# One encoder layer with a Fourier mixer and a gated convolutional FFN on one core: first weight sums by accumulating DMA, subtractions moved from GpSimd to VectorE, earlier weight folds, fewer transfers in the down projection, and another split of the last norm

## The chip, the cores and the metric

The kernel runs on one core of one Trainium2 chip. The metric is the device time of one execution in microseconds, the median of several runs.

The engines go by the names of the profile: PE is TensorE (matmuls), DVE is VectorE, ACT is ScalarE, POOL is GpSimd, SP is the engine that only issues transfers. Each runs its own list of instructions in order and waits on semaphores where it needs another's result. A transfer is issued from SP's, ACT's or POOL's list and then runs by itself; only those issued from POOL can add to what stands in the destination ("accumulating").

## What is computed

The input x is 1024 positions by 1024 channels, float32, batch 1, one layer:

```python
def reference(x, ...):
    h = layer_norm(x, emb_ln_g, emb_ln_b)
    mix = fourier_mixer(h, fn_w_in, fn_b_in, fn_w_out, fn_b_out)
    h = layer_norm(DEEPNORM_ALPHA * h + mix, ln_tok_g, ln_tok_b)
    ffn = conv_ffn(h, ff_w_up, ff_conv_w, ff_conv_b, ff_w_down)
    return layer_norm(DEEPNORM_ALPHA * h + ffn, ln_ffn_g, ln_ffn_b)

def fourier_mixer(x, w_in, b_in, w_out, b_out):
    h = (x @ w_in + b_in).reshape(bsz, s, FN_GROUPS, FN_GROUP_DIM)
    f = jnp.fft.fft2(h, axes=(1, 3), norm="ortho").real
    return f.reshape(bsz, s, FN_WIDTH) @ w_out + b_out

def conv_ffn(x, w_up, conv_w, conv_b, w_down):
    h = depthwise_conv(x @ w_up, conv_w, conv_b)      # 3 taps over positions
    g, v = jnp.split(h, 2, axis=-1)                   # 2816 columns each
    return (jax.nn.silu(g) * v) @ w_down
```

## The kernel before

**Numbers in two pieces.** Each float32 operand of a matmul is split into a high part and a low part, both in the type float32r. `split` is a cast on ACT (high) and a subtraction `lows` on DVE or POOL (source minus high), and `mm3` multiplies in three passes: low × high, high × low, high × high (lines 190, 192, 194). So every product needs two operands, each with a high and a low part, and a low part is a tensor_tensor over the whole operand.

**Stages.** (1) Norm of x, transposes, the input weights with the transform over channels folded in, and the first products. (2) The transform over positions: `dft_cos` and `dft_sin` multiply with tables `ct` and `sn`. Their results come as banks `bp` and `bq` of PSUM and are split into `pte`, `pt` and `qt`. The output weights are used as sums and differences of mirrored columns ("folds"): `fold_load` fetches two pieces `w1` and `wd`, `fold_sums` negates `wd` on ACT and lets two accumulating transfers from POOL add the other piece to each, and `fold_split` splits the result into `wf`. A last piece, the weights' end rows with the biases, is `wee_f`, cast to `wee`. (3) For four row blocks t of positions, `out_sin` and `out_cos` multiply with the folded weights, `out_ln` adds the residual and takes the norm of row blocks t and t + 4 (statistics on DVE, a power on POOL, called `z10rs` and so on, and the centring), and `out_turn` transposes into `v` (PE), with gain and bias applied by ACT, or half by DVE where `both` is set. (4) The up projection: 22 column tiles j, each as seven products in the manner of Strassen, `prod(j, i)` with operands `a{i}_{j}` (weights: the columns `wr` and their sums `s`) and `b{i}` (activations: `v` and their differences `s1v`, `s2v`, `s4v`), collected in banks bx, by and bz and added up on DVE as `c`. Then three taps, the gate and a store to DRAM (`gd`). (5) The down projection: seven products s, each over six quads b of the inner dimension. Its operands are fetched by `down_load`, added to by `down_pile` (a negation on ACT, accumulating transfers from POOL), and split by `down_prep`. (6) The last norm, `last_row` and `finish`, for eight row blocks, 4 to 7 first and 3 last.

**What sets the order.** PE, DVE, ACT and POOL run their instructions in the order in which the code is written. SP's transfers are ordered by a scheduler. Tiles come from pools with a fixed number of slots: tag `t4` (46 slots of 4 KB for each partition), `t2` (7 slots of 2 KB) and `small` (24); a new tile waits until the last reader of the slot's former tile is done.

**The places that the change touches.** In stage 2, `wee_f` is loaded after the loop over t, and its cast on ACT stands ahead of the copies of the first `bp` banks. Between stages 3 and 4, the products of j = 0 and j = 1 are interleaved with the last `out_ln` and `out_turn`, by hand. There `prep_sums` makes four sums for each j on POOL (s5 = w2a + w2b, s6 = s5 − w1a, s7 = w1a − w2a, s3 = w1b − s6, with w1 and w2 the two weight tiles of j and a, b their halves), and part of the `lows` is given to POOL as well. In stage 5 the operand of s = 3 is made of `qw`, negated, plus the tile `sb`, by an accumulating transfer from tile to tile. In stage 6, `finish` divides each row: a part of the columns is normed by ACT and POOL, the rest by DVE.

Of the kernel before, what the change touches and what calls it, by code (L numbers as in the profile page):

```python
# [152 lines left out]
def encoder_layer(ctx: ExitStack, tc: tile.TileContext, a, out: bass.AP):  # L153
# [426 lines left out]
    pair_center(1)  # L580
    for t in range(4):
# [36 lines left out]
        if t == 2:  # L618
# [8 lines left out]
            for i in (2, 3):  # L627
                fold_load(i)

    wee_f = t4([82, D], F32, "wee_f")  # L630
    nc.sync.dma_start(out=wee_f, in_=a["we"])
# [355 lines left out]
    out_ln(
        3,
        between=lambda: prep_b(5, ca, nc.gpsimd, part=(1,)),
        late=lambda: prep_b(6, ca, part=(1,)),  # L990
    )
# [28 lines left out]
    prep(0, (7,), nc.gpsimd)  # L1020
    for k2 in range(2):
        t = t4([P, 2, 512], F32, f"s4v{k2}")
        nc.gpsimd.tensor_tensor(out=flat(t), in0=flat(v21[k2]), in1=flat(s2v[k2]), op=ALU.subtract)
# [390 lines left out]
```

## Time and profile before

| what | value |
|---|---|
| median of 3 runs | 865.66 us (863.42 to 867.71) |
| the profiled execution | 865.14 us, span 863.4 us, mean granted clock 0.974 |
| PE busy | 815.2 us, 94% of the span |
| DVE busy | 688.9 us, 80% |
| ACT busy | 391.9 us |
| POOL busy | 325.8 us |
| moved by transfers | 120.71 MB, mean 140 GB/s |

The profiled execution is one run with a recorder; its time lies between those of the three runs. Windows of the span give the busy time of each engine in a stretch; the granted clock is the share of full speed at which PE was let run there. A row of the waits names the engine, the array and line that waited, then the engine, array and line that released it. A row of the timeline gives start and length in us, then engine, line, operation and tiles; brackets at its end give the idle time before it and who ended it. Stage 2 lies at about 82 to 116 us, the passage from stage 3 to 4 at about 115 to 225, the loop over j until about 630, stage 5 until the end of the matmuls at 847, and the last norm in the last 45 us.

### The profile page before, as it was taken

The numbers are of one execution on the slowest core, as the hardware profiler recorded it, in microseconds if no ns is written. First come the engines' busy times: TensorE is split into PE (matmuls) and PEld (weight loads), VectorE is DVE, ScalarE is ACT, GpSimd is POOL, SyncE is SP. The second block draws the span as 40 slices with busy tenths as digits, with TensorE's granted clock in tenths as the row PEclk, the third lists the DMA queues.
The fourth block names the chain that finished last, engine by engine and source line by source line (L and its number), as shares of the span: only waits on it lengthen the run. The fifth ranks groups of instructions, "written<-read, shape, count | busy, mean of one in ns | idle before, by whom it ended". The sixth has DMA issues, their size and how long they took to land.

```text
span 863.4 us, 10465 instructions
## 1 busy us (share of the span) xinstructions
PE 815.2 (94%) x3816; PEld 671.3 (78%) x3816; DVE 688.9 (80%) x998; ACT 391.9 (45%) x592; POOL 325.8 (38%) x239
## 2 busy tenths in 40 slices
PE   9999899968899999999999999999999988999992
PEld 7889778867788788888888888888878866788882
DVE  4995588999888998888788888887897865678755
ACT  5535523564254443443444343443645744466311
POOL 4303100487535444545444444543052322310075
PEclk9999899997999999999999999999999999999996
DMA  9428821312024222222232222224889999999022
GB/s 363 141 67 212 190 87 73 123 49 88 11 80 136 78 73 74 74 74 73 86 113 95 74 74 74 73 74 165 324 282 212 244 268 242 263 298 334 38 98 98
DMA packets 38266, 120.71 MB, mean 140 GB/s; under 512 B 4358, under 2 KB 5254, under 8 KB 38214
## 3 DMA queue, kind: packets, MB, share of 16 engines
q1 hardware_dynamic: 22966, 79.05, 26.0%
q0 software_dynamic: 8912, 29.45, 17.3%
q10 hardware_dynamic: 6336, 11.54, 3.5%
q8 instruction: 30, 0.49, 0.2%
q14 instruction: 22, 0.18, 0.1%
HBM read 94.33 MB, written 19.92 MB: 132 GB/s over the span
## 4 chain that ended last, share of the span: by engine, by line
PE 52%; DVE 15%; issue 14%; DMA 8%; POOL 6%; ACT 3%; POOLq 0%; ACTq 0%; DVEq 0%
PE by L190 6%; PE by L192 6%; PE by L194 6%; PE bz L190 4%; PE bz L194 4%; PE bz L192 4%; PE bx L190 4%; PE bx L194 4%; PE bx L192 4%; DMA qa<-sa 3%; DMA wee_f<-we 2%; DMA qa<-gd 2%; DVE b L181 2%; DVE t L1039 1%; POOL acc L1272 1%
## 5 line engine op out<-in xcount | busy, mean ns | idle before, releaser
L1074 POOL TENSOR_TENSOR t<-t,t 128x1024 f32<-128x1024 f32 x22 | 54.6, 2480 | 241.3 <-DVE t L1039 177.1
L1039 DVE SCALAR_TENSOR_TENSOR t<-c,cols,t 128x1 f32<-128x1 f32 (+2 forms) x264 | 142.0, 586 | 3.7 <-ACT t L1064 0.5
L190 PE MATMUL by<-b,a 128*128 128x512 f32 (+1 forms) x268 | 106.9, 399 | 4.7 <-DVE c L918 2.7
L192 PE MATMUL dn<-wb,ga 128*128 128x512 f32 x264 | 105.3, 399 | 4.7 <-DVE wb L181 2.4
L190 PE MATMUL dn<-wb,ga 128*128 128x512 f32 x264 | 104.8, 397 | 3.8 <-DVE ga L181 2.2
L192 PE MATMUL by<-b,a 128*128 128x512 f32 (+1 forms) x268 | 106.3, 397 | 1.1 <-DVE b L181 1.1
L194 PE MATMUL by<-b,a 128*128 128x512 f32 (+1 forms) x268 | 105.9, 395 | 0.0
L194 PE MATMUL dn<-wb,ga 128*128 128x512 f32 x264 | 104.3, 395 | 0.0
L181 DVE TENSOR_TENSOR a<-s,a 128x512 fp32r<-128x512 f32 x85 | 89.9, 1057 | 15.1 <-ACT a L869 14.9
L192 PE MATMUL bz<-b,a 128*128 128x512 f32 (+1 forms) x180 | 70.7, 393 | 3.3 <-DVE b L181 3.3
L190 PE MATMUL bx<-b,a 128*128 128x512 f32 (+1 forms) x192 | 72.2, 376 | 0.5 <-ACT c L982 0.5
L194 PE MATMUL bx<-b,a 128*128 128x512 f32 (+1 forms) x192 | 71.9, 375 | 0.0
L192 PE MATMUL bx<-b,a 128*128 128x512 f32 (+1 forms) x192 | 71.9, 375 | 0.0
L190 PE MATMUL bz<-b,a 128*128 128x512 f32 (+1 forms) x180 | 71.1, 395 | 0.0
L181 DVE TENSOR_TENSOR a<-wr,a 128x512 fp32r<-128x512 f32 x64 | 69.6, 1090 | 1.6 <-ACT a L869 1.6
L194 PE MATMUL bz<-b,a 128*128 128x512 f32 (+1 forms) x180 | 70.8, 393 | 0.0
L190 PEld LDWEIGHTS by<-b,a 128*128 128x128 f32 x268 | 51.6, 192 | 17.3 <-DVE c L918 3.9
L192 PEld LDWEIGHTS dn<-wb,ga 128*128 128x128 f32 x264 | 50.0, 189 | 18.4 <-DVE wb L181 3.9
L190 PEld LDWEIGHTS dn<-wb,ga 128*128 128x128 f32 x264 | 49.9, 189 | 16.7 <-ACT wb L184 2.6
L192 PEld LDWEIGHTS by<-b,a 128*128 128x128 f32 x268 | 51.6, 193 | 12.6 <-DVE b L181 1.3
L918 DVE TENSOR_TENSOR c<-bz,c 128x512 f32<-128x512 f32 x44 | 30.4, 691 | 38.9 <-PE bz L194 38.1
L194 PEld LDWEIGHTS by<-b,a 128*128 128x128 f32 x268 | 51.5, 192 | 11.6
(350 smaller groups left out, 1838.8 us busy)
## 6 DMA issues: line engine op xcount, KB each, us to landing
wr<-wup SPq DMA_DIRECT2D x44, 512.0 KB
gd<-t ACTq DMA_DIRECT2D x44, 256.0 KB
qa<-gd SPq DMA_DIRECT2D x20, 512.0 KB
sa<-gd POOLq DMA_DIRECT2D x15, 512.0 KB, 15.6
sb<-wd POOLq DMA_DIRECT2D x15, 512.0 KB, 11.7
qw<-wd SPq DMA_DIRECT2D x15, 512.0 KB
winT<-winT SPq DMA_DIRECT2D x8, 512.0 KB
x<-x SPq DMA_DIRECT2D x8, 512.0 KB
```

What stands on the lines that cost most here:

```text
L181: eng.tensor_tensor(out=lo, in0=src, in1=raw(hi), op=ALU.subtract)
L190: nc.tensor.matmul(outs[i], ll, rh[i], start=first, stop=False, **kw)
L192: nc.tensor.matmul(outs[i], lh, rl[i], start=False, stop=False, **kw)
L194: nc.tensor.matmul(outs[i], lh, rh[i], start=False, stop=last, **kw)
L918: nc.vector.tensor_tensor(out=o, in0=b, in1=x, op=ALU.add)
L1039: nc.vector.scalar_tensor_tensor(out=t[:, lo:hi], in0=c[:, lo + sh : hi + sh], scalar=w[:, wi : wi + 1], in1=t[:, lo:hi], op0=ALU.mult, op ...
L1074: nc.gpsimd.tensor_tensor(out=tg, in0=tg, in1=tv, op=ALU.mult)
L1272: nc.gpsimd.tensor_tensor(out=z[:, d], in0=z[:, d], in1=ffg[:, d], op=ALU.mult)
```

## The change

**A. Folds and `wee_f` earlier.** The loads of folds 0 and 1 go ahead of the loop over t, the sums of 0 and 1 and the loads of 2 and 3 and of `wee_f` behind its step t = 0, the sums of 2 and 3 behind t = 1. On ACT, the place around the cast of `wee`, before and then after:

```order
L184 CAST ge31_929<-ve3_927 128x520
L184 CAST go30_968<-vo3_967 128x504
L184 CAST go31_970<-vo3_967 128x504
L534 ACTIVATE wd_2_866<-wd_2_866 126x1024
L534 ACTIVATE wd_3_870<-wd_3_870 126x1024
L696 CAST wee_978<-wee_f_976 82x1024
L662 CAST pte_861<-bp00_993 16x258
```

```order
L184 CAST wf000_931<-wd_0_356 126x1024
L184 CAST ge30_936<-ve3_935 128x520
L184 CAST ge31_937<-ve3_935 128x520
L184 CAST go30_976<-vo3_975 128x504
L184 CAST go31_978<-vo3_975 128x504
L696 CAST wee_984<-wee_f_531 82x1024
L664 CAST pte_877<-bp00_993 16x258
```

The two negations of `wd_2` and `wd_3` (L534) no longer stand between the last cast of stage 1 and that of `wee`; they stand some 30 rows further ahead.

**B. Sums by transfers, lows on DVE.** For j = 0 and 1, three and two of the sums are now loaded as one weight half (from SP), negated on ACT where needed (`sums_turn`), and completed by accumulating transfers from POOL (`sums_pile`); `s3` and `s7` of j = 1 are made by DVE. The `lows` that POOL had there, and `s4v`, go to DVE. `out_turn(2)` no longer gives half of its scalings to DVE. The weights of j = 1 are loaded earlier. On POOL, the passage from stage 3 to 4, before and then after (L223 are the powers of the norm; the old code calls the tiles of s5, s6, s7 and s3 of j = 0 `s0_0` to `s3_0`, the new one `s5_0` and so on):

```order
L858 TENSOR_TENSOR s0_0_1558<-wr01_1224 128x512
L851 TENSOR_TENSOR s1_0_1559<-s0_0_1558,wr00_1222 128x512
L223 TENSOR_TENSOR z10rs_1571<-z10v_1570,small_70 128x1
L181 TENSOR_TENSOR a5_0_1586<-s0_0_1558,a5_0_1586 128x512
L181 TENSOR_TENSOR a6_0_1589<-s1_0_1559,a6_0_1589 128x512
L223 TENSOR_TENSOR z11rs_1603<-z11v_1602,small_70 128x1
L181 TENSOR_TENSOR a1_1_1706<-wr10_1638,a1_1_1706 128x512
L181 TENSOR_TENSOR a2_1_1709<-wr10_1638,a2_1_1709 128x512
L223 TENSOR_TENSOR z30rs_1769<-z30v_1768,small_70 128x1
L181 TENSOR_TENSOR b501_1731<-s1v0_1648,b500_1730 128x2x256
L181 TENSOR_TENSOR b511_1733<-s1v1_1649,b510_1732 128x2x256
L223 TENSOR_TENSOR z31rs_1783<-z31v_1782,small_70 128x1
```

```order
L872 DMA s6_0_1228<-wup 128x512
L223 TENSOR_TENSOR z20rs_1493<-z20v_1492,small_70 128x1
L223 TENSOR_TENSOR z21rs_1507<-z21v_1506,small_70 128x1
L872 DMA s6_1_1454<-wup 128x512
L872 DMA s5_1_1456<-wup 128x512
L223 TENSOR_TENSOR z10rs_1590<-z10v_1589,small_70 128x1
L223 TENSOR_TENSOR z11rs_1616<-z11v_1615,small_70 128x1
L872 DMA s6_1_1454<-wup 128x512
L223 TENSOR_TENSOR z30rs_1765<-z30v_1764,small_70 128x1
L223 TENSOR_TENSOR z31rs_1794<-z31v_1793,small_70 128x1
L858 TENSOR_TENSOR s0_2_2113<-wr21_2083 128x512
```

The subtractions of 512 columns are gone from between the powers; accumulating transfers stand there, one of them ahead of `z30rs`, and the next tensor_tensor behind `z31rs` is the first sum of j = 2. On DVE, the place ahead of the low of `a5_1`, which the product into bank bz1 reads, before and then after:

```order
L181 TENSOR_TENSOR b611_1739<-s2v1_1651,b610_1738 128x2x256
L181 TENSOR_TENSOR a6_1_1948<-s1_1_1873,a6_1_1948 128x512
L898 TENSOR_TENSOR v001_1207<-v101_1211,v001_1207 128x1024
L898 TENSOR_TENSOR v011_1209<-v111_1213,v011_1209 128x1024
L181 TENSOR_TENSOR a5_1_2008<-s0_1_1872,a5_1_2008 128x512
L181 TENSOR_TENSOR b701_2012<-v001_1207,b700_2011 128x1024
L181 TENSOR_TENSOR b711_2014<-v011_1209,b710_2013 128x1024
```

```order
L181 TENSOR_TENSOR b611_1782<-s2v1_1661,b610_1781 128x2x256
L181 TENSOR_TENSOR a6_1_1954<-s6_1_1454,a6_1_1954 128x512
L1044 TENSOR_TENSOR s7_1_1957<-wr10_1450,wr11_1452 128x512
L880 TENSOR_TENSOR s3_1_1959<-wr10_1450,s6_1_1454 128x512
L915 TENSOR_TENSOR v001_1207<-v101_1211,v001_1207 128x1024
L915 TENSOR_TENSOR v011_1209<-v111_1213,v011_1209 128x1024
L181 TENSOR_TENSOR a7_0_2011<-s7_0_1226,a7_0_2011 128x512
L1054 TENSOR_TENSOR s4v0_2014<-v100_1210,s2v0_1660 128x1024
L1054 TENSOR_TENSOR s4v1_2016<-v110_1212,s2v1_1661 128x1024
L181 TENSOR_TENSOR a5_1_2018<-s5_1_1456,a5_1_2018 128x512
L181 TENSOR_TENSOR b701_2022<-v001_1207,b700_2021 128x1024
L181 TENSOR_TENSOR b711_2024<-v011_1209,b710_2023 128x1024
```

Five operations that POOL had (`s7_1`, `s3_1`, `a7_0`, and the two of `s4v`) now stand between `a6_1` and `a5_1`.

**C. Down projection.** At s = 3 the negation of `qw` and the accumulating transfer `qw<-sb` are gone; `down_prep` subtracts on DVE instead (`sb` minus `qw`, in place). The tile `sa` of s = 1 is fetched when the matmuls of s = 0 are issued (`early`). On POOL, the accumulating transfers of s = 3, before and then after:

```order
L1088 DMA qa30_5729<-sa0_5267 128x1024
L1088 DMA qw30_5731<-sb0_4962 128x1024
L1088 DMA qa31_5771<-sa1_5311 128x1024
L1088 DMA qw31_5773<-sb1_5087 128x1024
L1088 DMA qa32_5812<-sa2_5352 128x1024
L1088 DMA qw32_5814<-sb2_5091 128x1024
L1088 DMA qa33_5853<-sa3_5391 128x1024
L1088 DMA qw33_5855<-sb3_5205 128x1024
L1088 DMA qa34_5894<-sa4_5430 128x1024
L1088 DMA qw34_5896<-sb4_5209 128x1024
```

```order
L1119 DMA qa30_5739<-sa0_5235 128x1024
L1119 DMA qa31_5781<-sa1_5287 128x1024
L1119 DMA qa32_5820<-sa2_5334 128x1024
L1119 DMA qa33_5859<-sa3_5375 128x1024
L1119 DMA qa34_5899<-sa4_5414 128x1024
L1119 DMA qa35_5925<-sa5_5453 128x512
```

The six `qa` transfers now follow each other.

**D. Last norm.** Each row block takes two scalar_tensor_tensor operations of 1024 columns on DVE; only row block 3 leaves 224 columns to ACT (scale) and POOL (bias), and stores them from ACT's queue.

The pool `t2` has 8 slots instead of 7, `small` 18 instead of 24. The core of the diff:

```diff
+    for i in range(2):
+        fold_load(i)
     for t in range(4):
...
         if t == 0:
             bias_block()
-            for i in range(2):
+        if t < 2:
+            for i in (2 * t, 2 * t + 1):
+                fold_sums(i)
+        if t == 0:
+            for i in (2, 3):
                 fold_load(i)
+            wee_f = t4([82, D], F32, "wee_f")
+            nc.sync.dma_start(out=wee_f, in_=a["we"])
...
+    def sums_load(j, which):
+        for i, v, h in which:
+            t = sums[j][i] = t2([P, 512], F32, f"s{i}_{j}")
+            nc.sync.dma_start(out=t, in_=a["wup"][j, v, :, hs[h]])
+
+    def sums_pile(j, which):
+        for i, v, h in which:
+            nc.gpsimd.dma_start(out=sums[j][i], in_=a["wup"][j, v, :, hs[h]], accum_op=ALU.add)
+
+    def sums_turn(j, i):
+        nc.scalar.mul(sums[j][i], sums[j][i], -1.0)
+
+    def sums_last(j):
+        o = sums[j]
+        o[3] = t2([P, 512], F32, f"s3_{j}")
+        nc.vector.tensor_tensor(out=o[3], in0=raws[j][0][:, 512:], in1=o[6], op=ALU.subtract)
...
     load_up(0)
+    sums_load(0, ((7, 1, 0), (6, 0, 0), (5, 1, 0)))
     out_sin(0)
     sin_adds(0)
     recenter(1)
+    sums_turn(0, 7)
+    sums_turn(0, 6)
+    sums_pile(0, ((7, 0, 0), (6, 1, 0), (5, 1, 1)))
...
-    out_turn(2, 0, True)
+    out_turn(2, 0)
...
-    prep_sums(0, (0,))
...
-        prep(0, (5, 6), nc.gpsimd)
...
-    prep(0, (7,), nc.gpsimd)
+    prep(0, (7,))
     for k2 in range(2):
         t = t4([P, 2, 512], F32, f"s4v{k2}")
-        nc.gpsimd.tensor_tensor(out=flat(t), in0=flat(v21[k2]), in1=flat(s2v[k2]), op=ALU.subtract)
+        nc.vector.tensor_tensor(out=flat(t), in0=flat(v21[k2]), in1=flat(s2v[k2]), op=ALU.subtract)
...
-    prep_b(4, full, nc.gpsimd)
+    prep_b(4, full)
...
         elif s == 3:
-            negate(xb, b)
             pile(xa, sst[b][:, 0:n])
-            pile(xb, tst[b][:, 0:n])
...
+        if s == 3:
+            nc.vector.tensor_tensor(out=xb[:, 0:n], in0=tst[b][:, 0:n], in1=xb[:, 0:n], op=ALU.subtract)
...
-        nb = st([P, 1], F32, f"nb{i}")
         nc.vector.scalar_tensor_tensor(
-            out=z[:, c], in0=z[:, c], scalar=mv[:, 0, 0:1], in1=ffg[:, c], op0=ALU.subtract, op1=ALU.mult
+            out=z, in0=z, scalar=mv[:, 0, 0:1], in1=ffg, op0=ALU.subtract, op1=ALU.mult
         )
...
+        pieces = (slice(0, 1024),) if i != 3 else (slice(0, 400), slice(400, 800))
+        if i == 3:
+            d = slice(800, 1024)
+            nc.scalar.activation(out=z[:, d], in_=z[:, d], func=AF.Identity, scale=rs)
+            nc.gpsimd.tensor_tensor(out=z[:, d], in0=z[:, d], in1=ffb[:, d], op=ALU.add)
+        for e in pieces:
             nc.vector.scalar_tensor_tensor(
                 out=z[:, e], in0=z[:, e], scalar=rs, in1=ffb[:, e], op0=ALU.mult, op1=ALU.add
             )
...
```

More of the change, by code (lines that the diff above doesn't have):

```diff
@@ L168, in st @@
     def st(shape, dt, name):
-        return pool.tile(shape, dt, name=name, tag="small", bufs=24)
+        return pool.tile(shape, dt, name=name, tag="small", bufs=18)
     def bank(name):
@@ L626, in encoder_layer @@
             nc.gpsimd.dma_start(out=pte[80:82], in_=a["c_one"][3:5])
[L627 to L631, printed above, removed]
     wee = t4([82, D], F32R, "wee")
@@ L977, in encoder_layer @@
     out_cos(3, 1)
-    prep(1, (1, 2), nc.gpsimd)
+    prep(0, (5, 6), part=(0,))
     bx[0], by[0], bz[0] = [bank(n) for n in ("bx0", "by0", "bz0")]
@@ L982, in encoder_layer, with ahead_b, ahead_c @@
     nc.scalar.copy(out=cc[0][0][:, ca], in_=bx[0][:, ca])
-    prep_b(5, ca, part=(0,))
-    prep_b(6, ca, part=(0,))
+    prep(1, (1, 2), part=(0,))
     out_turn(1, 1)
[L987 to L991, printed above, removed]
+    def ahead_b():
+        bsums(vcols(2), nc.vector, (0, 1))
+        prep(1, (1,), part=(1,))
+        prep_b(5, ca, part=(0,))
+        prep_b(6, ca, part=(0,))
+    def ahead_c():
+        prep(0, (5, 6), part=(1,))
+    out_ln(3, between=ahead_b, late=ahead_c)
+    prep_b(5, ca, part=(1,))
+    prep_b(6, ca, part=(1,))
+    prep(1, (2,), part=(1,))
     bx[1] = bank("bx1")
@@ L1000, in encoder_layer @@
     prod(0, 6, by[0], True, True, ca)
-    prep_sums(1, (0,))
     prep_b(1, cb)
-    prep_b(2, cb, nc.gpsimd)
-    prep_sums(0, (1,))
-    prep_sums(1, (1,))
+    prep_b(2, cb)
+    sums_last(0)
     out_turn(3, 1, True)
@@ L1014, in encoder_layer @@
     prep(1, (6,))
+    sub7 = sums[1][7] = t2([P, 512], F32, "s7_1")
+    nc.vector.tensor_tensor(out=sub7, in0=raws[1][0][:, 0:512], in1=raws[1][1][:, 0:512], op=ALU.subtract)
+    sums_last(1)
     bsums(full, nc.vector, (2,))
@@ L1197, in encoder_layer @@
         if j == 0:
-            prep_b(3, full, nc.gpsimd, ks=(1,))
+            prep_b(3, full, ks=(1,))
         if j == NF - 1:
@@ L1269, in finish @@
             )
-            if i == 3:
-                nc.sync.dma_start(out=out[rc, e], in_=z[:, e])
-        nc.gpsimd.tensor_tensor(out=z[:, d], in0=z[:, d], in1=ffg[:, d], op=ALU.mult)
-        nc.gpsimd.tensor_tensor(out=z[:, d], in0=z[:, d], in1=ffb[:, d], op=ALU.add)
-        if i != 3:
-            nc.sync.dma_start(out=out[rc], in_=z)
-        else:
-            nc.sync.dma_start(out=out[rc, d], in_=z[:, d])
+            nc.sync.dma_start(out=out[rc, e], in_=z[:, e])
+        if i == 3:
+            nc.scalar.dma_start(out=out[rc, d], in_=z[:, d])
     order = [(s, b) for s in range(7) for b in range(NB)]
```

28 lines of the change are left out of this document (12 added, 16 removed).

## The prediction

> **What bounds the kernel now.** I read the page's busy table first, then windows along the span, then TensorE's waits, then the chain and the timeline where the waits stand.
>
> The page, busy us, share of the span, instructions; then windows (start:end, length, busy us of each engine with its instructions, granted TensorE clock, DMA share, GB/s):
>
> ```profile
> PE 815.2 (94%) x3816; PEld 671.3 (78%) x3816; DVE 688.9 (80%) x998; ACT 391.9 (45%) x592; POOL 325.8 (38%) x239
> ...
> 80.00:100.00 20.00, 16.17 (x101) 14.27 (x100) 9.27 (x21) 6.52 (x10) 6.01 (x9) 0.97 0.89 192
> 100.00:120.00 20.00, 19.86 (x103) 16.06 (x102) 16.99 (x25) 13.25 (x31) 0.00 (x0) 0.86 0.52 174
> ...
> 160.00:180.00 20.00, 14.43 (x89) 12.88 (x88) 19.66 (x37) 13.25 (x30) 9.63 (x9) 0.94 0.37 131
> 180.00:200.00 20.00, 15.55 (x114) 15.15 (x113) 19.16 (x21) 8.55 (x18) 19.06 (x12) 0.89 0.08 30
> 200.00:220.00 20.00, 15.75 (x54) 12.18 (x53) 19.96 (x15) 9.01 (x12) 14.94 (x7) 0.79 0.30 104
> ...
> 720.00:740.00 20.00, 17.18 (x68) 13.41 (x67) 11.19 (x14) 7.28 (x8) 5.64 (x9) 0.91 1.05 263
> ```
>
> TensorE is the bound; only its holes can be won. They stand in four places, and each belongs to one part of the change: 80–100 with slow matmuls behind it, 160–220 (there VectorE is full: 58.8 of 60 us), 720–740 with full DMA engines, and the tail. TensorE's waits by releaser (total, times, longest); the first and third lie in 160–220, the second in 80–100, the last in 720–740:
>
> ```profile
> PE tt L826 <- DVE xr L227: 5.1, 1, 5.1
> PE bp L190 <- ACT pte L664: 3.8, 1, 3.8
> PE bz L192 <- DVE b L181: 3.3, 1, 3.3
> ...
> PE dn L190 <- DVE ga L181: 2.2, 1, 2.2
> ```
>
> **Part A, `wee_f` and the folds earlier.** The chain of waits (start, us), and ACT's timeline:
>
> ```profile
> 82.32 13.89 DMA wee_f<-we
> 96.28 1.05 ACT wee L696
> ...
> 114.31 0.61 DVE qt L181
> ...
> 89.35 2.00 ACT L534 ACTIVATE wd<-wd 126x1024 f32<-126x1024 f32 x2
> ```
>
> The cast of `wee` waits until 96.28 for a transfer issued at 82.32, and ACT's copies of the first `bp` banks stand behind it; TensorE, out of banks, loses the 3.8 us above. From the cast on ACT and VectorE work without a pause to the last `qt` at 114.92, which starts out_sin(0). The new order issues `wee_f` after t = 0 and moves both negations of 2.00 us in front of it to earlier steps, so the cast starts where the negations start now, at 89.35: 96.28 − 89.35 = 6.9 us. The 3.8 us wait and the slow clock behind it lie inside these 6.9 and aren't added: 3.83 lost in 80–100 and, at a granted 0.86, 0.14 × 19.86 = 2.8 in 100–120 make 6.6. Moved DMAs count too: on SP four fold loads come earlier, on POOL the four first piles now stand ahead of `x3rs`, which by my walk they still leave in time. **A: −7**, bounds −3.8 (the wait alone) and −7.
>
> **Part B, first sums by DMA, lows to VectorE.** VectorE's and POOL's timelines (start, us, form, count):
>
> ```profile
> 145.56 1.41 DVE L751 SCALAR_TENSOR_TENSOR xr<-xr,sw,bv 128x512 f32<-128x512 f32 x2 [1.97 <-PE bv L194]
> ...
> 168.49 0.42 DVE L898 TENSOR_TENSOR s1v<-v,v 128x256 f32<-128x256 f32 x1
> 168.95 1.38 DVE L898 TENSOR_TENSOR s2v<-v,s1v 128x256 f32<-128x256 f32 x1
> 171.80 0.43 DVE L898 TENSOR_TENSOR s2v<-v,s1v 128x256 f32<-128x256 f32 x1
> ...
> 181.98 1.36 DVE L835 TENSOR_SCALAR v<-tt,cols 128x128 f32<-128x128 f32 x4
> ...
> 194.80 4.54 DVE L181 TENSOR_TENSOR b<-s2v,b 128x512 fp32r<-128x512 f32 x2
> ...
> 202.02 2.35 DVE L898 TENSOR_TENSOR v<-v,v 128x1024 f32<-128x1024 f32 x2
> ...
> 212.83 2.89 DVE L181 TENSOR_TENSOR a<-s,a 128x512 fp32r<-128x512 f32 x1
> ...
> 224.19 0.68 DVE L918 TENSOR_TENSOR c<-by,c 128x512 f32<-128x512 f32 x1
> ...
> 168.56 2.91 POOL L181 TENSOR_TENSOR a<-wr,a 128x512 fp32r<-128x512 f32 x2 [5.68 <-ACT a L869]
> 195.98 5.57 POOL L1023 TENSOR_TENSOR s4v<-v,s2v 128x1024 f32<-128x1024 f32 x2
> 212.31 2.85 POOL L181 TENSOR_TENSOR b<-v,b 128x1024 fp32r<-128x1024 f32 x1
> ```
>
> VectorE's 256-column subtraction takes 0.42 us until POOL's tensor_tensor starts at 168.56, then 1.38, and 0.43 when POOL is done. A 512-column operation takes 0.68 at 224.19, where POOL is between its own, and a low 2.89 under POOL's at 212.83. So VectorE is full because POOL stretches it. From the start of the first to the start of the last of these VectorE rows, 101 instructions in the order of the program, lie 78.6 us. With each form at its spacing where POOL is idle (0.60 us for 512 columns, 1.13 for 1024) they add up to 52 us; 26 us are stretch and short waits.
>
> Moved to VectorE are 5 lows of `a` and 4 of `b` at 0.6, 3 lows of `b` with 1024 columns at 1.13, `s4v` (2 × 1.13), and `s7_1`, `s3_0`, `s3_1` at 0.6: 9 × 0.6 + 5 × 1.13 + 3 × 0.6 = 12.9 us. Taken from VectorE are 8 scalings of row block 2 at 1.36/4 = 0.34: −2.7 (ACT has room: 13.25 and 8.55 of 20). So it needs 52 + 12.9 − 2.7 = 62 us where it had 78.6. POOL keeps only 1-column powers and DMA issues until the sums of j = 2.
>
> I walked the new order with these durations, from the start that A gives. Centring of the last row block comes 10.6 us earlier than now (A's 7 in it), prod(0,4) at 201.7 against 218.59, 16.9 earlier. That is 10 for B. A new wait is priced in it: bz1's product now waits some 2 us for the low of `a5_1`, which stands behind `s7_1`, `s3_1`, `a7_0` and `s4v` on VectorE. Shorter idle time also gives clock back (0.89 and 0.79 granted now). **B: −10.5**. Bounds: no more than VectorE's gain, −16.4; at the other end −3, if the order on VectorE keeps TensorE waiting as it does now.
>
> The accumulating transfers: `s6` of j = 1 needs a load, ACT's negation and two piles in sequence, and its second pile stands ahead of `z30rs` on POOL, for which the centring and the transposes wait. By my walk that has 5 us of slack. No 256 KB pile is in the trace. The nearest, with full DMA engines (median us to landing):
>
> ```profile
> qa<-sa POOLq DMA_DIRECT2D x5, 512.0 KB, 15.0
> ...
> qw<-sb POOLq DMA_DIRECT2D x1, 256.0 KB, 10.5
> ```
>
> At 10.5 each the chain just fits; the DMA share here is 0.37 and less, so I take it as hidden: 0, bounds 0 and +8 (one pile at 15.0 more than fits). The Trainium skill, "DMA: Bandwidth & Descriptors", section "Anatomy of one DMA — SWDGE (gpsimd) path", fits such a transfer as 2.0 us + bytes/436 GB/s; by that, an estimate, a pile takes 2.6 us and nothing is late; the rows above stand far over it, so I don't sum by it. The Trainium skill also speaks against this part: "SBUF — State Buffer", section "SBUF: two separate sides", says that a VectorE operation in a two-port mode locks POOL out of writing its descriptors; that would delay a pile behind a VectorE centring. No run here shows it.
>
> **Part C, fewer transfers in the down projection.** POOL's and TensorE's timelines:
>
> ```profile
> 703.88 0.88 POOL L1088 DMA_DIRECT2D qw<-sb  x1 [5.36 <-ACT qw L1091]
> ...
> 712.11 1.16 POOL L1088 DMA_DIRECT2D qa<-sa  x1
> ...
> 733.27 0.47 PE L190 MATMUL dn<-wb,ga 128*128 128x512 f32 x1 [2.24 <-DVE ga L181]
> 734.32 0.79 PE L192 MATMUL dn<-wb,ga 128*128 128x512 f32 x1 [0.58 <-DVE wb L181]
> ```
>
> At stage s = 3 each `qw<-sb` pile waits for ACT's negation, and the `qa` piles behind it on POOL wait too: `qa32`'s leaves at 712.11, lands some 15–18 us later, and its split is late at 733.27. Without the `qw` piles it leaves about 9 us earlier (behind the first `qa`), and six transfers of 2.75 MB go. One VectorE subtraction of 1.13 us per quad replaces negation and pile; VectorE has 11.19 of 20 there. The hole of 730–735 is worth 2.8 us of idle time (17.18 of 20) and 0.09 × 17.18 = 1.5 of slow clock, 4.3 us. Late next: the waits of 0.8 us at s = 2, which come before and stay. **C: −4.3**, bounds 0 (another pile takes its place) and −7.
>
> **Part D, the last norm on VectorE.** The chain in the tail, the last matmul, and the full-width form:
>
> ```profile
> 846.87 0.28 PE L194 MATMUL dl<-wb,ga 128*128 128x256 f32 x1
> ...
> 851.40 0.41 DVE L1391 TENSOR_TENSOR acc<-acc,dl 128x256 f32<-128x256 f32 x1
> ...
> 847.62 1.26 POOL L1273 TENSOR_TENSOR acc<-acc,ffb 128x512 f32<-128x512 f32 x1
> ...
> 852.29 1.26 POOL L1273 TENSOR_TENSOR acc<-acc,ffb 128x512 f32<-128x512 f32 x1
> 853.51 1.33 POOL L223 TENSOR_TENSOR o3rs<-o3v,small 128x1 f32<-128x1 f32 x1
> ...
> 856.68 0.59 POOL L1273 TENSOR_TENSOR acc<-acc,ffb 128x192 f32<-128x192 f32 x1
> ...
> L333 DVE SCALAR_TENSOR_TENSOR xr<-xr,sw,embg 128x1024 f32<-128x1024 f32 x4 | 4.9, 1277 | 0.0
> ```
>
> Matmuls end at 847.15, but row block 3's last add comes at 851.40, since each row block before it takes 4.7 us in a ring POOL–VectorE–ACT–POOL (852.29 − 847.62). With two full-width operations of 1.28 us a block takes VectorE 2.9 us (4–7) or 4.3 (0–2, with add and statistics), so it is free at about 844, and row block 3 starts at 847.2: 0.41 + 0.43 + 0.4, then the first operation beside `o3rs` until 849.9, ACT's 224 columns 0.6, POOL's add 0.9 at most, issue at 851.4 on ACT's queue. Now the last issue is at 857.3 (right after the last POOL row). **D: −5.9**, bounds −5 (POOL's operations slow) and −6.5. The smaller pool of small tiles and the eighth `t2` slot I cost at nothing: the readers of a reused small tile are long done, and `nb` is gone.
>
> **Sum.** −7 − 10.5 − 4.3 − 5.9 = −27.7. The profiled execution took 865.14 us (span 863.4): 837.4. Its time is 0.5 below the median of 865.66, so 838.
>
> **Rivals.** (1) The order keeps TensorE waiting: for the low of `a5_1` and for VectorE's additions B gives 3 instead of 10.5: 845. For it: more work stands on VectorE ahead of each product. Against: 16.4 us less in all. (2) C is hidden: DMA stays at 1.05 and the next pile is late; 842. (3) The pile chain of `s6_1` is late by more than its slack and holds `z30rs`: B becomes about 0 to +3, 848 to 851. Against it stand 5 us of slack and DMA engines two thirds free; no row excludes it: 1 in 20. (4) The other side: the stretch doesn't leave with POOL's work. Then the 26 us stay, and the moved 12.9 us stretch as the lows at 194.80 do (2.27 against 0.68, 3.3 times): +43 − 2.7 = +40, and with A, C and D (−17.2) the time is 889. It turns slower once the moved operations take over 19.9 us, 1.55 times their own. The rows at 168.49–171.80, which turn with POOL's, speak against it.
>
> **Chances.** As summed 0.62; (1) 0.18; (2) 0.11; (3) 0.05; (4) 0.04. Bounds of the likeliest: −7 − 16.4 − 7 − 6.5 = −37 gives 829; the small ends of C and D with B as taken, 843. The range reaches to case (3): 828 to 851. A difference under 0.5% (4.3 us) can't be told from no change: faster 0.95, same 0.02, slower 0.03.
>
> **What would show it.** A: `wee`'s cast at 89–90 and no wait of TensorE at `bp`; out_sin(0) near 108. B: VectorE lows of 512 columns at 0.68 between 150 and 200, no wait at `tt` beyond 1 us, 200–220 busy over 18 of 20. C: no idle over 1 us at 720–740. D: last issue at most 4.5 us behind the last matmul. Wrong would make me: 256 KB piles landing after 15 us and more, lows that stay over 1.5 us, a wait at `bz` over 4 us, or a late load of j = 2 (its slots now wait for VectorE's `s4v`).

## The result and the profile after

The changed kernel takes 840.37 us (median of four runs, 836.84 to 840.92) against 865.45 us (863.42 to 867.71) for the kernel before, a ratio of 0.9701 with a 95% interval of 0.9665 to 0.9737 (formed from all runs of both, so not exactly the quotient of the medians). The profiled execution took 840.92 us, with a span of 839.2 us at a mean granted clock of 0.989; the forecast was 838 us, with a range of 828 to 851. Two single executions in the experiments below took about 1609 us, one of the kernel before and one of the changed kernel; all times and ratios leave them out.

First the page's busy table of the changed kernel, then windows of the span with the columns that they had before:

```profile
PE 807.3 (96%) x3816; PEld 665.1 (79%) x3816; DVE 691.8 (82%) x1005; ACT 385.0 (46%) x590; POOL 273.3 (33%) x203
...
80.00:100.00 20.00, 20.00 (x136) 18.20 (x135) 14.76 (x31) 10.87 (x22) 2.51 (x5) 1.00 0.43 139
100.00:120.00 20.00, 19.90 (x100) 15.28 (x100) 15.82 (x23) 7.84 (x21) 2.67 (x3) 1.00 0.70 208
...
160.00:180.00 20.00, 15.36 (x113) 14.28 (x112) 19.11 (x40) 12.41 (x30) 1.52 (x2) 0.91 0.13 54
180.00:200.00 20.00, 17.15 (x94) 14.71 (x94) 19.96 (x24) 13.22 (x20) 5.07 (x3) 0.91 0.25 80
200.00:220.00 20.00, 17.08 (x67) 13.43 (x66) 17.26 (x20) 5.53 (x8) 9.80 (x6) 0.91 0.08 26
...
720.00:740.00 20.00, 20.00 (x88) 16.25 (x87) 19.43 (x21) 16.59 (x19) 2.53 (x3) 1.00 1.03 259
```

The matmul count is the same, and TensorE is still the bound. 80–120 and 720–740 are now all but without holes and at full clock. In 160–220 TensorE is busy for 49.6 us, where it was 45.7: better, but this is where holes remain. VectorE stays full up to 200 although POOL has little to do before 195: VectorE now does POOL's work in the time that it used to lose.

TensorE's waits (total, times, longest) say which holes are left:

```profile
PE bz L190 <- DVE a L181: 4.1, 2, 2.9
PE by L190 <- DVE c L935: 3.3, 2, 2.9
...
PE tt L826 <- DVE xr L227: 0.2, 1, 0.2
```

The 5.1 us at the transposes (`tt`) have become 0.2, those at `bp` are gone from the list, and so are the 2.2 us for the split of `qa32`. In their place stand a wait for the low of `a5_1` (bz, 2.9) and one for an addition `c` (by, 2.9). Smaller waits stand beside them: 1.7 us in two at bx, 1.2 at bz, and 1.5 at bz for a low of `b`, where that one was 3.3.

For an account by place, I took for every matmul of both traces the distance to the next one's start, less the usual distance for its form, and added up what is over. That counts idle time and slow clock together. What is taken as usual is a choice, which moves a difference by up to some 0.4 us.

| place | lost before, us | lost after, us | difference | the forecast's term |
|---|---|---|---|---|
| 90–120 (A) | 8.0 | 1.0 | −7.0 | −7 |
| 160–225 (B) | 22.7 | 16.4 | −6.3 | −10.5 |
| 620–740 (C) | 12.3 | 7.5 | −4.8 | −4.3 |
| last matmul to the end (D) | 16.2 | 10.7 | −5.5 | −5.9 |
| whole span | | | −24.2 | −27.7 |

The four places give −23.6 of the span's −24.2 (863.4 to 839.2). Three terms hold to within about half a microsecond; B is some 4 us short.

### The profile page after: what moved, and what is told of

The parts are those of the page before. It is cut to its first block, busy times and chain, and to the rows that moved or that the text cites. A ratio compares the mean times of both kernels' runs of the same rounds, so it can differ in the third digit from the quotient of the medians.

```text
span 839.2 us, 10434 instructions
## 1 busy us (share of the span) xinstructions
PE 807.3 (96%) x3816; PEld 665.1 (79%) x3816; DVE 691.8 (82%) x1005; ACT 385.0 (46%) x590; POOL 273.3 (33%) x203
## 4 chain that ended last, share of the span: by engine, by line
PE 58%; DVE 7%; DMA 5%; issue 4%; POOL 3%; ACT 1%; DVEq 0%; SPq 0%; POOLq 0%; ACTq 0%
PE by L190 7%; PE by L194 6%; PE by L192 6%; PE bz L190 4%; PE bz L192 4%; PE bz L194 4%; PE dn L192 4%; PE dn L194 4%; PE dn L190 4%; PE bx L190 4%; PE bx L194 4%; PE bx L192 4%; DMA sb<-wd 4%; DVE acc L1298 1%; DVE a L181 1%
## 5 line engine op out<-in xcount | busy, mean ns | idle before, releaser
L181 DVE TENSOR_TENSOR a<-s,a 128x512 fp32r<-128x512 f32 x88 | 87.5, 995 | 14.8 <-ACT a L886 14.5
L190 PEld LDWEIGHTS by<-b,a 128*128 128x128 f32 x268 | 50.8, 189 | 15.9 <-DVE c L935 4.7
L192 PEld LDWEIGHTS dn<-wb,ga 128*128 128x128 f32 x264 | 49.6, 188 | 17.2 <-DVE wb L1188 3.3
L1256 ACT COPY c<-bx 128x512 f32<-128x512 f32 x22 | 12.9, 588 | 106.6 <-DVE c L935 106.6
L190 PEld LDWEIGHTS dn<-wb,ga 128*128 128x128 f32 x264 | 49.6, 188 | 13.9 <-ACT wb L1187 2.3
L194 PEld LDWEIGHTS by<-b,a 128*128 128x128 f32 x268 | 50.6, 189 | 11.7
```

What stands on the lines that cost most here:

```text
L181: eng.tensor_tensor(out=lo, in0=src, in1=raw(hi), op=ALU.subtract)
L190: nc.tensor.matmul(outs[i], ll, rh[i], start=first, stop=False, **kw)
L192: nc.tensor.matmul(outs[i], lh, rl[i], start=False, stop=False, **kw)
L194: nc.tensor.matmul(outs[i], lh, rh[i], start=False, stop=last, **kw)
L1256: nc.scalar.copy(out=cg[:, 0:512], in_=bx[j])
```

## The experiments

The kernel before took 865.4 to 867.1 us on the chips of these runs, so each kernel is compared with it by the ratio on its own chip.

**Each part alone.** The first four kernels are the kernel before with one part of the change each.

`only_a`:

```diff
+    for i in range(2):
+        fold_load(i)
     for t in range(4):
...
+        if t < 2:
+            for i in (2 * t, 2 * t + 1):
+                fold_sums(i)
+        if t == 0:
+            for i in (2, 3):
+                fold_load(i)
+            wee_f = t4([82, D], F32, "wee_f")
+            nc.sync.dma_start(out=wee_f, in_=a["we"])
```

> The kernel before with part A alone (folds and wee_f earlier, everything else as before). Theory from the two traces: the TensorE time lost at 90 to 120 us falls from 8.0 to 1.0 us and all behind it moves, so 7.0 us faster than before, the cast of wee near 89.6, the first matmul of out_sin(0) that waits for qt3 near 108 us. Rival: the passage at 160 to 220 is bound by something that A does not move (loads of wr, the sums on POOL) and gives part back: 2 to 4 us faster.

Measured: 0.9908 (0.9895 to 0.9921), 8.0 us less (6.9 to 9.1). The term of −7 lies in the interval.

`only_b` is the whole of part B, of which this is the kind of edit:

```diff
+    sums_load(0, ((7, 1, 0), (6, 0, 0), (5, 1, 0)))
...
+    sums_pile(0, ((7, 0, 0), (6, 1, 0), (5, 1, 1)))
...
-        prep(0, (5, 6), nc.gpsimd)
...
-    prep(1, (1, 2), nc.gpsimd)
+    prep(0, (5, 6), part=(0,))
```

> The kernel before with part B alone (sums of j = 0 and 1 by accumulating transfers, lows and s4v on VectorE, row block 2's scalings on ACT, the two pool sizes). Theory from the two traces: B is worth 6.3 us, what TensorE's lost time at 160 to 225 us fell by (22.7 to 16.4). The recorded sum said 10.5. Rival: B needs A's earlier start for its transfers or is worth nothing by itself: within 2 us of before.

Measured: 0.9914 (0.9896 to 0.9931), 7.5 us less (6.0 to 9.0). The whole interval lies below the term of 10.5. TensorE's waits of this kernel:

```profile
PE bp L190 <- ACT pte L664: 5.3, 1, 5.3
PE bz L190 <- DVE a L181: 4.0, 2, 2.8
PE by L190 <- DVE c L935: 3.6, 2, 3.2
```

The two waits that the changed kernel has at bz and by stand here with about the same size, so they belong to B and not to its meeting with the other parts. (The wait at `bp` is 1.5 us longer than before: the cast of `wee` had to wait for `wee_f` until 98.13 us here, where it was 96.28.)

`only_c`:

```diff
         elif s == 3:
-            negate(xb, b)
             pile(xa, sst[b][:, 0:n])
-            pile(xb, tst[b][:, 0:n])
...
+        if s == 3:
+            nc.vector.tensor_tensor(out=xb[:, 0:n], in0=tst[b][:, 0:n], in1=xb[:, 0:n], op=ALU.subtract)
```

> The kernel before with part C alone (no qw<-sb transfer and no negation at s = 3, a VectorE subtraction instead, sa fetched earlier). Theory: 4.8 us faster (lost time at 620 to 740 us from 12.3 to 7.5), no TensorE wait over 1 us at 725 to 740. The recorded term was 4.3. Rival: the gain of after in this stretch comes from the earlier phase of the transfers that A and B brought; alone C gives 0 to 2 us.

Measured: 0.9927 (0.9914 to 0.9941), 6.3 us less (5.1 to 7.5), somewhat more than expected. Between 680 and 770 us no wait of TensorE over 0.8 us is left in it.

`only_d`:

```diff
-        nc.scalar.activation(out=z[:, d], in_=z[:, d], func=AF.Identity, scale=rs, bias=nb)
...
-        nc.gpsimd.tensor_tensor(out=z[:, d], in0=z[:, d], in1=ffg[:, d], op=ALU.mult)
-        nc.gpsimd.tensor_tensor(out=z[:, d], in0=z[:, d], in1=ffb[:, d], op=ALU.add)
...
+        pieces = (slice(0, 1024),) if i != 3 else (slice(0, 400), slice(400, 800))
```

> The kernel before with part D alone (last norm on VectorE). Theory: 5.5 us faster, the time from the last matmul to the end of the span 10.8 us instead of 16.3. The recorded term was 5.9. Rival: the stores of the rows pile up at the end, and the span ends as late as before: 0 to 2 us.

Measured: 0.9921 (0.9905 to 0.9936), 6.9 us less (5.5 to 8.2); its tail from the last matmul to the end is 10.5 us.

The four alone make −28.7 us. The whole, by its ratio of 0.9701, makes −25.9 (−22.8 to −29.0). With some 1.2 to 1.5 us of uncertainty on each part, the difference of 2.8 can't be told from none: within what these runs resolve, the parts add up.

**What B lacks: POOL's sums of j = 2, or the order on VectorE?** VectorE's rows in the changed kernel, and POOL's sums:

```profile
188.83 2.35 DVE L1054 TENSOR_TENSOR s4v<-v,s2v 128x1024 f32<-128x1024 f32 x2
191.10 0.68 DVE L181 TENSOR_TENSOR a<-s,a 128x512 fp32r<-128x512 f32 x1
...
194.57 2.35 DVE L181 TENSOR_TENSOR b<-s4v,b 128x1024 fp32r<-128x1024 f32 x2
...
198.58 1.79 DVE L181 TENSOR_TENSOR a<-wr,a 128x512 fp32r<-128x512 f32 x1
...
201.99 2.28 DVE L181 TENSOR_TENSOR b<-v,b 128x1024 fp32r<-128x1024 f32 x1
204.19 0.68 DVE L935 TENSOR_TENSOR c<-by,c 128x512 f32<-128x512 f32 x1
...
194.85 3.26 POOL L858 TENSOR_TENSOR s<-wr 128x512 f32<-128x512 f32 x1 [25.91 <-ACT b L905]
198.19 1.63 POOL L851 TENSOR_TENSOR s<-s,wr 128x512 f32<-128x512 f32 x1
```

and the two waits of TensorE behind them:

```profile
191.84 0.79 PE L190 MATMUL bz<-b,a 128*128 128x512 f32 x1 [2.85 <-DVE a L181]
204.92 0.50 PE L190 MATMUL by<-b,a 128*128 128x512 f32 x1 [2.92 <-DVE c L935]
```

Up to 197 us a low of 512 columns takes 0.68 us, as the forecast had it. The first of POOL's sums of j = 2 starts at 194.85 and itself takes 3.26 us, while VectorE's two lows beside it keep their 1.18 each. From then on POOL's sums take 1.63 and more, and VectorE's operations 1.8 us for 512 columns and 2.28 for 1024; the addition `c` that prod(0,4) needs comes at 204.19. My theory was that this stretch, which the forecast's walk did not have, makes the wait at by; the rival, that the order of VectorE's operations does, since five of them stand ahead of the low of `a5_1`. The changed kernel was measured again on the chip of the next three:

> The changed kernel itself, on the same chip as the next three, so that they can be compared with it: ratio to before 0.970, some 25 us faster.

Measured: 840.14 us, 0.9711 (0.9685 to 0.9737).

`late` holds the sums of j = 2 back until the addition is done, by a copy of one column on POOL:

```diff
         if j == 0:
+            gate = cpool.tile([P, 1], F32, name="gate")
+            nc.gpsimd.tensor_copy(out=gate, in_=cv[:, 1023:1024])
             prep_sums(2)
```

> The changed kernel, with POOL's four sums of j = 2 held back until VectorE has written c01 (a one-column copy on POOL in front of them). Theory, that what B fell short by comes from these sums, which start at 194.9 us and stretch the six VectorE operations ahead of c01 by 3.9 us: c01 is done near 201 instead of 204.9, TensorE's wait of 3.3 us there goes, with its slow clock 3 to 4 us faster than the changed kernel. Rival, that VectorE is simply behind by its own work: the wait only moves behind 205 us (bx2, by2), within 1 us of the changed kernel.

Measured: 839.32 us, 0.9688 (0.9670 to 0.9707). POOL's and VectorE's timelines, and the window that held the wait:

```profile
201.51 1.11 POOL L1252 COPY gate<-c 128x1 f32<-128x1 f32 x1 [32.76 <-DVE c L935]
...
197.69 0.69 DVE L181 TENSOR_TENSOR a<-wr,a 128x512 fp32r<-128x512 f32 x1
...
200.03 0.68 DVE L935 TENSOR_TENSOR c<-by,c 128x512 f32<-128x512 f32 x1
...
202.49 2.40 DVE L181 TENSOR_TENSOR a<-wr,a 128x512 fp32r<-128x512 f32 x2
...
200.00:220.00 20.00, 20.00 (x88) 16.18 (x87) 19.07 (x23) 5.53 (x8) 13.85 (x9) 1.00 0.07 24
```

With POOL still, the same operations take 0.69 us, the addition comes at 200.03 instead of 204.19, and TensorE is busy for all of 200–220, at full clock. The product prod(0,4) starts at 201.40 instead of 204.92. So the stretch is what made the wait at by: that much is shown. In TensorE's account some 2 to 3 us go from 160–260, though part of what the sums' delay costs is lost later in that stretch (new waits for an addition at 224, 234 and 254 us). On the whole time the intervals of `late` and of the changed kernel overlap.

`order` puts VectorE's operations in the order in which the products need them (`a5_1` first, then `a7_0`; `s4v`, `s3_1` and the low half of `b4` later):

```diff
     prep(1, (6,))
-    sub7 = sums[1][7] = t2([P, 512], F32, "s7_1")
-    nc.vector.tensor_tensor(out=sub7, in0=raws[1][0][:, 0:512], in1=raws[1][1][:, 0:512], op=ALU.subtract)
-    sums_last(1)
+    prep(1, (5,))
...
         if j == 0:
-            prep_b(3, full, ks=(1,))
+            prep_b(4, full, part=(1,))
+            prep(0, (3,))
+            prep_b(3, full)
+            sums_last(1)
```

> The changed kernel with VectorE's order at 184 to 205 us by need: the low of a5_1 directly behind that of a6_1, then a7_0, s7_1 and b7, c01's additions ahead of b4's lows, s3_1 last. Theory: the wait of 3.2 us at bz1 goes; the wait for c01 becomes one for b4 at about 200 to 202 us, since POOL's sums still stretch it: 2 to 4 us faster than the changed kernel. Rival, that VectorE's sum of work alone sets the end and the order nothing: 0 to 1 us.

Measured: 837.78 us, 0.9679 (0.9665 to 0.9693). The wait of 2.85 us for `a5_1` is gone. New ones stand some 8 us later (TensorE's timeline):

```profile
199.56 0.53 PE L190 MATMUL by<-b,a 128*128 128x512 f32 x1 [2.06 <-DVE c L935]
201.32 0.79 PE L192 MATMUL by<-b,a 128*128 128x512 f32 x1 [1.24 <-DVE b L181]
```

`order_late` joins both; its gate reads a low of `b3` instead of `c`.

> Both: VectorE's order by need, and POOL's sums of j = 2 held back until the low of b30 is written. Theory: the product (0, 4) starts near 199 us instead of 204.9, so 5 to 7 us faster than the changed kernel, 833 to 835 us where that takes 840. Rival: the lows of j = 2 come too late for by2, and 2 to 3 us of it are lost again.

Measured: 839.0 us, 0.9689 (0.9676 to 0.9701), no better than either. VectorE's timeline, and TensorE's longest wait in 160–260:

```profile
204.10 0.69 DVE L880 TENSOR_TENSOR s<-wr,s 128x512 f32<-128x512 f32 x1
...
211.64 1.13 DVE L181 TENSOR_TENSOR a<-s,a 128x512 fp32r<-128x512 f32 x1 [0.57 <-ACT a L886]
...
PE by L190 <- DVE a L181: 3.2, 1, 3.2
```

VectorE runs without stretch until 204; but now the sums of j = 2 are late, and the low of `a6_2`, made from one of them, holds TensorE for 3.2 us.

`sums_dve` is `order` with the two sums of j = 2 that are needed first made by VectorE, and the other two held back on POOL until the low of `a6_2`:

```diff
-            prep_sums(2)
             prep(2, (1,))
...
+            nc.vector.tensor_tensor(out=s5, in0=w2[:, 0:512], in1=w2[:, 512:], op=ALU.add)
+            nc.vector.tensor_tensor(out=s6, in0=s5, in1=w1[:, 0:512], op=ALU.subtract)
```

> VectorE's order by need as in the run order, with the first two sums of j = 2 made by VectorE (0.6 us each) and POOL's other two held back until the low of a6_2 is written, and s3_1 and the lows of a4_1 and a3_1 behind it. Theory: no POOL operation reads SBUF between 169 and 208 us, so the product (0, 4) starts near 199 us and by2's waits at most 1 us: 6 to 8 us faster than the changed kernel, 832 to 835 us where that takes 840. Rival, that VectorE's order costs elsewhere what it gains: 836 to 838 us, as order and order_late did.

Measured: 838.9 us, 0.9705 (0.9681 to 0.9729). prod(0,4) starts at about 201, and a new wait stands further back:

```profile
228.57 0.80 PE L190 MATMUL by<-b,a 128*128 128x512 f32 x1 [3.60 <-DVE c L935]
```

Four ways of removing a wait of 3 us left the time at 837.8 to 839.3 us, where the changed kernel had 840.4 and 840.1. By the ratios they gain 0.5 to 2.8 us on it, each with an uncertainty of some 3 us. `order` alone came out as it was expected to; the other three fell short of the 3 to 8 us expected of them. Each wait went where the edit took it away, and another came 5 to 30 us later. `order` has the lowest ratio, but its interval overlaps that of the changed kernel, so it isn't shown to be the better one. What the waits have in common is VectorE, which releases every one of them and is busy for 75.2 to 78.1 of the 80 us of 160–240 in all five kernels. That its work as a whole sets this passage, and the order decides only which product waits, fits all five; it is my reading and not shown: no run took work off VectorE there, the kernel before has the same 75.9 of 80 with more time lost, and some further order that avoids all the waits isn't excluded.

**Does POOL's reading stretch VectorE?** That the stretch would leave with POOL's work carried most of B. Two kernels put work back on POOL that nobody uses. `pool_reads` adds twelve subtractions of two tiles in SBUF behind the last low of `a2_1`, `pool_writes` nine memsets at the same place:

```diff
+    idle = sums[0][5]
+    for _ in range(12):
+        nc.gpsimd.tensor_tensor(out=idle, in0=raws[0][0][:, 0:512], in1=raws[0][1][:, 0:512], op=ALU.subtract)
```

```diff
+    for _ in range(9):
+        nc.gpsimd.memset(idle, 0.0)
```

> The changed kernel with twelve subtractions of 512 columns more on POOL, from 168.6 us on, which read two weight tiles and write a tile that nobody reads any more. No result changes. Theory, that VectorE was stretched by POOL's tensor_tensors: VectorE's operations with two SBUF operands between 169 and 188 us take 1.2 to 2.9 us instead of 0.68, the low of a5_1 comes 8 to 12 us later, and so does the end: 848 to 853 us. Rival, that the stretch in the kernel before had another source (transfers, ACT): rows of 0.68 as before, within 1 us of the changed kernel.

> The same place, but nine memsets of the same tile on POOL, which read nothing. No result changes. The Trainium skill, SBUF — State Buffer, section Who interferes with whom, says that a VectorE operation with two SBUF operands contends with a POOL operation that reads SBUF and not with one that only writes; by it the time is that of the changed kernel within 1 us, and VectorE's rows stay at 0.68. Rival, that any busy POOL stretches VectorE: 8 us and more slower, as with the reads.

Measured: `pool_reads` 851.52 us, 0.9833 (0.9813 to 0.9853); `pool_writes` 840.76 us, 0.9718 (0.9695 to 0.9740). The timelines of POOL and VectorE, of the reads first (the second and third row are two of POOL's twelve, by themselves):

```profile
169.98 21.96 POOL L1024 TENSOR_TENSOR s<-wr,wr 128x512 f32<-128x512 f32 x12
...
174.76 1.60 POOL L1024 TENSOR_TENSOR s<-wr,wr 128x512 f32<-128x512 f32 x1
...
181.47 4.21 POOL L1024 TENSOR_TENSOR s<-wr,wr 128x512 f32<-128x512 f32 x1
...
170.12 1.76 DVE L227 TENSOR_SCALAR xr<-xr,zmv,z31rs 128x1024 f32<-128x1024 f32 x1
171.80 3.43 DVE L181 TENSOR_TENSOR b<-s1v,b 128x512 fp32r<-128x512 f32 x2
175.15 3.43 DVE L181 TENSOR_TENSOR b<-s2v,b 128x512 fp32r<-128x512 f32 x2
...
180.17 1.36 DVE L835 TENSOR_SCALAR v<-tt,cols 128x128 f32<-128x128 f32 x4
181.46 2.48 DVE L181 TENSOR_TENSOR b<-v,b 128x512 fp32r<-128x512 f32 x4
```

and of the writes:

```profile
169.14 5.61 POOL L1024 MEMSET s<- 128x512 f32 x9
...
170.12 1.27 DVE L181 TENSOR_TENSOR b<-s1v,b 128x512 fp32r<-128x512 f32 x2
171.32 1.28 DVE L181 TENSOR_TENSOR b<-s2v,b 128x512 fp32r<-128x512 f32 x2
```

Under POOL's reads these VectorE lows take 1.71 us (3.43 for two), under its memsets 0.64 as with POOL idle. The scalings at 180.17, which read PSUM, take the same 0.34 each as in the kernel before. The memsets cover 5.6 us only, the reads 22, so the two totals are not a like comparison; the single rows are. The reads cost about 11 us of the whole, more than the 6 to 7.5 that B gains.

The rows say more than that VectorE gets slower. While the two alternate, a VectorE operation lasts about as long as the POOL operation beside it, whatever its own size: 1.71 us beside 1.60 here, and in the rows of the prediction 1.38 us for 256 columns beside POOL's 1.45 (2.91 for two) and 2.89 for 512 columns beside POOL's 2.85. And it is not always VectorE that is held: at 181.46, behind the scalings, four lows in a row take 0.62 us each, as with POOL quiet, while the one POOL subtraction beside them takes 4.21. So what I called a stretch reads as a wait for the other engine's operation, and not as a factor. The 3.26 us of POOL's first sum in the changed kernel is of the same kind. The memsets bring none of it. This agrees with the Trainium skill, "SBUF — State Buffer", section "Who interferes with whom", which says that a VectorE instruction with two inputs in SBUF contends with a GpSimd instruction that reads SBUF, and not with one that only writes it.

**C: the place in POOL's queue, the bytes, or the negation?** `pile_order` is the kernel before with the piles `qw<-sb` of s = 3 two quads later on POOL: the same transfers, another order, so that the `qa` piles no longer wait behind a `qw` pile and its negation.

```diff
             pile(xa, sst[b][:, 0:n])
-            pile(xb, tst[b][:, 0:n])
+            held_back.append((xb, tst[b][:, 0:n]))
+            for args in held_back[: max(0, len(held_back) - 2)] if b < NB - 1 else held_back:
+                pile(*args)
```

> The kernel before with the same transfers and negations at s = 3, but each qw pile issued two quads later on POOL, so that the qa piles of the next two quads don't stand behind it. Theory, that part C's gain is the place in POOL's queue: the qa32 pile leaves before 705 us instead of 712.1 and TensorE's wait at 730 to 735 us goes: 3 to 5 us faster than before. Rival, that it is the 2.75 MB and six transfers that C removes: within 1 us of before, the wait stays or moves to a qw operand.

Measured: 870.76 us, 1.0054 (1.0036 to 1.0073), 4.7 us more. POOL and TensorE:

```profile
705.34 0.87 POOL L1088 DMA_DIRECT2D qw<-sb  x1 [2.92 <-ACT qw L1091]
...
725.24 0.79 PE L190 MATMUL dn<-wb,ga 128*128 128x512 f32 x1 [3.84 <-ACT wb L184]
```

The `qa32` pile left 10.6 us earlier (701.55 against 712.11) and the wait for its split all but went, as meant. Now the pile of the first quad's `qw`, issued at 705.34, lands at 724.05, where in the kernel before it was issued at 703.88 and landed at 716.9, and TensorE waits 3.84 us for the split of that. The DMA share is 1.05 to 1.07 in 680–740 in both kernels: with the engines full, an earlier landing of one operand was paid for by a later one of another. So the theory fails. The rival was right that a wait moves to a `qw` operand, but it expected the time to stay. As the `qw` piles still had to land here, the run doesn't say what the place is worth where they are gone.

What C takes away besides the piles is ACT's negation of `qw`. ACT's timeline of the kernel before, and the pile of `qa32` there, show what held the split for which TensorE waited at 733.27:

```profile
729.81 1.06 ACT L1091 ACTIVATE qw<-qw 128x1024 f32<-128x1024 f32 x1 [6.07 <-DMA qw<-wd]
730.77 1.09 ACT L184 CAST ga<-qa 128x1024 fp32r<-128x1024 f32 x1
...
L1088 POOL DMA_DIRECT2D qa<-sa x1: 1158/1158/1158, 712.1 to 712.1; - x1
DMA to landing us min/median/max: 14.2/14.2/14.2
```

The pile landed at 726.35, 14.2 us after its issue, but the cast of `qa32` started only at 730.77. It stands in ACT's list behind the negation of `qw34`, the tile of two quads later, and ACT sat idle for 6.07 us until that tile's load was there. The 4.4 us between landing and cast are more than TensorE's wait of 2.24. In `only_c` the negation is gone, the pile leaves at 703.67 and lands at 721.89, and the cast starts at 724.45.

C has also 2.89 MB less to move (117.82 MB in `only_c` against 120.71), about 11 us of transfer at the 257 GB/s of 690–740, and an earlier fetch of `sa`. The trace shows that the negation held the split; no run takes the negations, the bytes or the fetch away alone, so how the 6.3 us divide stays open.

## Why the prediction was right, and where it was not

The total came within 2.4 us of the forecast, and the sign and the range held. Behind it three terms hold in size and one is some 4 us short; of the three, C's holds for another cause than the one named. By its steps:

- **A: right in mechanism and size.** The cast of `wee` was to stand at 89–90, and out_sin(0) near 108. ACT's timeline has the cast at 89.61, and the matmuls of out_sin(0) that read the last `qt` start at 108.22; no wait at `bp` is left.

```profile
89.61 1.04 ACT L696 CAST wee<-wee_f 82x1024 fp32r<-82x1024 f32 x1
```

- **B: right in mechanism, mis-sized: −6.3 in the account and −7.5 alone where the term was −10.5.** The walk held for most of the way: VectorE's lows stayed at 0.68 up to 197 us, the transposes waited for 0.2 us, and the low of `a5_1` came at 191.10. The step that failed is "prod(0,4) at 201.7": it started at 204.92, so 13.7 us earlier than before instead of 16.9, and less A's 7 that makes 6.7. The walk priced VectorE as unstretched all the way there and POOL as quiet "until the sums of j = 2", and did not put a time on those; they began at 194.85. With them held back in `late`, prod(0,4) starts at 201.40. The wait for `a5_1`, priced at some 2 us, was 2.85; with 1.2 more at bz it touches the sign "a wait at `bz` over 4 us" in sum only. Rival (1), B at −3, came about by half. The walk also ends too early: in `late` part of what was won at 201 is lost again behind it. "200–220 busy over 18 of 20" is the sign that failed (17.08), and the lows at 0.68 held to 197 instead of 200. Rival (4) took the stretch as a factor of 3.3; by the rows of `pool_reads` it reads as operations that each wait for one of POOL's.

- **The piles: right to cost them at nothing.** Seven accumulating transfers of 256 KB, from issue to landing in the changed kernel:

```profile
L872 POOL DMA_DIRECT2D s<-wup x7: 880/918/1547, 106.5 to 152.7; - x7
DMA to landing us min/median/max: 4.1/6.2/7.7
```

They stand between the estimate of 2.6 us by the formula of the Trainium skill ("DMA: Bandwidth & Descriptors", section "Anatomy of one DMA — SWDGE (gpsimd) path") and the 10.5 us of the nearest row; here the measurement decides. (The kernel before had a second pile of 256 KB, of 12.5 us; "no 256 KB pile is in the trace" holds for this passage only.) Rival (3), a late `s6_1`, did not come: its second pile was issued at 152.7 and so had landed by about 160, and the transposes waited for 0.2 us only. The lock that the Trainium skill describes ("SBUF — State Buffer", section "SBUF: two separate sides") between VectorE's two-port modes and POOL's descriptors left no late pile; no run looked for it.

- **Rival (4), that the stretch stays, is out** by the rows at 188.83 and 191.10 and by `pool_reads` and `pool_writes`: it comes and goes with POOL's reading of SBUF.

- **C: the size held (−4.8 for −4.3); the reason named is not what set the wait.** The 4.3 us were read off the hole itself, so they fit any cause that empties it; that the size came out is no support for the cause named. The forecast let `qa32`'s pile leave late behind the `qw` piles and land "some 15–18 us later", which makes its split late. It did land after 14.2 us, at 726.35; the split was late because ACT stood at the negation of a later tile until 730.77. The other part, that the pile leaves about 9 us earlier without the `qw` piles, held in `only_c` (703.67 against 712.11), where it brought the landing forward by 4.5. Alone, C gave 6.3 us (5.1 to 7.5), at the far side of its bounds of 0 to 7. Rival (2), another pile in its place, is what happened in `pile_order`, not in the change.

- **D: right (−5.5 for −5.9).** VectorE's, POOL's and ACT's last rows:

```profile
828.16 0.28 PE L194 MATMUL dl<-wb,ga 128*128 128x256 f32 x1
...
830.04 1.27 DVE L1289 SCALAR_TENSOR_TENSOR acc<-acc,omv,ffg 128x1024 f32<-128x1024 f32 x1
...
831.76 1.65 DVE L1298 SCALAR_TENSOR_TENSOR acc<-acc,o3rs,ffb 128x400 f32<-128x400 f32 x2 [0.44 <-POOL o3rs L223]
...
830.27 1.46 POOL L223 TENSOR_TENSOR o3rs<-o3v,small 128x1 f32<-128x1 f32 x1 [3.50 <-DVE o3v L222]
...
833.00 0.87 ACTq L1303 DMA_DIRECT2D out<-acc  x1
```

The last issue comes 4.55 us behind the last matmul's end at 828.45, just over the 4.5 that were forecast at most. The 0.44 us in which VectorE waits for `o3rs` were not in the sum: the power on POOL ends after the full-width operation beside it.

## What to carry to other kernels

Before giving VectorE more work, look at what its operations take while POOL is quiet: here POOL's tensor_tensor work cost VectorE more time than it saved, and moving it back paid even though VectorE was already the full engine. Where one engine is full through a whole passage, taking out one wait of 3 us brought at most some 2.8 us and none that is clear of the noise, since another product waited instead; price the passage to its end, not to the first product behind the wait. When an operand is late, follow it through every engine that handles it: `qa32` had landed 4.4 us before its cast could start, because an operation for a later tile stood ahead in ACT's list. And where the DMA engines are full, another order of the same transfers can choose only which operand is late, as `pile_order` did.
